# A two-layer hybrid-attention block on one core: silu(c) left in PSUM for the opening, rotary rows doubled in the latent heads, modulation steps regrouped

## The chip, the cores and the metric

The kernel runs on one core of one Trainium2 chip. A time is device microseconds of that core for one execution of the whole program. Engines go by the profile's names: PE is TensorE (PEld its weight loads), DVE VectorE, ACT ScalarE, POOL GpSimd, SP SyncE, which issues every DMA of this kernel.

## What is computed

Two layers over 512 positions of width 1024, batch 1. Each layer has a modulated norm, four groups of attention heads of four heads each, an output product, a second modulated norm and an MLP of 4096 columns with a squared ReLU; a plain norm ends the program. What the change touches is the modulation, the first norm, the latent heads (MLA) and the compressed branch (NSA). The modulation is six parts per layer, each 1024 numbers:

```python
silu(c) @ w_ada[l] + b_ada[l]        # parts 1 and 0: scale and shift of the first norm
h = x * rsqrt(mean(x*x) + 1e-6) * g * (1 + scale) + shift

def mla_mixer(z, q_norm_g, kv_norm_g, w_uq, w_ukv):
    cq, ckv, k_pe = split_last(z, [MLA_Q_RANK, MLA_KV_RANK, MLA_ROPE])     # 192, 128, 32
    q = heads(rmsnorm(cq, q_norm_g) @ w_uq, MLA_HEADS)                     # 4 heads of 64 + 32
    kv = heads(rmsnorm(ckv, kv_norm_g) @ w_ukv, MLA_HEADS)
    q = concatenate([q[..., :64], rope(q[..., 64:], pos)], axis=-1)
    k = concatenate([kv[..., :64], broadcast(rope(k_pe, pos))], axis=-1)
    v = kv[..., 64:]
    return causal_attention_blocks(q, k, v, (64 + 32) ** -0.5)

def compress(t, pos_emb, w1, w2):      # NSA: 31 blocks of 32 positions, stride 16
    blk = overlapping_blocks(t) + pos_emb
    return gelu(blk.reshape(B, n_cmp, 32 * 64) @ w1) @ w2
```

## The kernel before

Activations are kept transposed: 128 features on the partitions, 512 positions along the row, eight such tiles for the width of 1024. Every wide product is done in three: a float32 operand is split into a rounded half (`hi`) and the rest (`lo`), and TensorE adds hi x hi, lo x hi and hi x lo in one PSUM bank (lines 331 to 333 in `mm3`). For weights the split is `W._split`: ScalarE copies the raw tile to `whi` (L89) and GpSimd, or VectorE, subtracts to `wlo` (L91). The raw tiles come through four buffers, one DMA each, all in SyncE's queue; a load waits there until a buffer's last reader is done.

The scheduler of the language sets each engine's order when the program is built, from the order of the code, and each engine then works its list strictly in turn.

The opening (`start`) loads x, sums the squares of its eight tiles (ScalarE squares into PSUM, VectorE adds, `sqacc`), sums over partitions on TensorE (`nsum`), takes the power -0.5 on GpSimd (`rs`, L257) and spreads it over the partitions on TensorE (`rsb`). In parallel it makes the two modulation parts that the first norm needs. One modulation step (`ada_cols`, L188) multiplies a 128x1024 tile of weights with silu(c) in every partition, sums along the row and adds the bias: one column of `mod`. silu(c) is spread over the partitions by eight small products into PSUM (`cbp`, L173), and VectorE copies it to SBUF (`cb`, L177). For tile k of h: two steps, one `gs` (norm weight times 1 + scale, 128x1, L1116), one `ht` = x * gs * rsb (L1122), then on ScalarE `hhi` = ht + shift rounded (L1125), and `hlo` = the rest, on GpSimd for the first five tiles (L1128) and on VectorE for the last three (L1130). Five projections (`pss`, five PSUM banks) are accumulated as the tiles come, 120 products in all. After them comes `proj_N`, whose first product is L503.

The latent heads follow. `cq_evac` turns 32 rows of k_pe: cos on one copy, sin on another, an add, a split into rows 64 to 96 of `cq[1]`. `mla_k` writes one head's key halves `mkh` and `mkl`: 64 rows from the product and 32 rotary rows copied from `cq[1]` by VectorE casts (L755, L756). `mla_q` copies 64 rows, multiplies two sets of 32 rows by cos and sin and adds them (L769 to L772), and splits. Scores are products over 96 rows (L784 to L786). `softmax` is VectorE (bias and minimum, L536), ScalarE (exponential, L541), VectorE (reciprocal), a scaling; `pv` transposes on TensorE, splits on ScalarE and VectorE, and multiplies with v (L590, L591). `kcvc_evac` adds position embeddings to the 31 overlapping blocks on VectorE, eight instructions per layer (L669). Other modulation steps, one 512 KB weight tile each, are placed by hand after heads and projections of layer 0 (`ada_step`; `NOUT` says how many go behind each output product).

## Time and profile before

| | |
|---|---|
| three runs | 1318.11 us median (1315.22 to 1322.64) |
| the profiled execution | 1317.07 us, span 1315.3 us, mean granted clock 0.986 |
| TensorE busy | 1244.1 us, 95% of the span |
| VectorE, ScalarE, GpSimd busy | 725.4, 588.3, 512.9 us |

The span runs from the first to the last instruction of the core; the rest of the execution lies around it. A matmul's busy time is longer than the distance to the next, since they are pipelined. A row of the timeline reads: start, duration, engine, line, operation, output<-inputs, shapes, count, and in brackets the engine's idle time before it with what ended it. A row of a group reads: line, engine, operation, names, shapes, count | busy us, mean ns | idle before. A row of waits reads: total us, times, longest.

### The profile page before, as it was taken

The numbers are of one execution on the slowest core, as the hardware profiler recorded it, in microseconds if no ns is written. First come the engines' busy times: TensorE is split into PE (matmuls) and PEld (weight loads), VectorE is DVE, ScalarE is ACT, GpSimd is POOL, SyncE is SP. The second block draws the span as 40 slices with busy tenths as digits, with TensorE's granted clock in tenths as the row PEclk, the third lists the DMA queues.
The fourth block names the chain that finished last, engine by engine and source line by source line (L and its number), as shares of the span: only waits on it lengthen the run. The fifth ranks groups of instructions, "written<-read, shape, count | busy, mean of one in ns | idle before, by whom it ended". The sixth has DMA issues, their size and how long they took to land. (4 is left out here: it accounts for less than half of the span.)

```text
span 1315.3 us, 17552 instructions
## 1 busy us (share of the span) xinstructions
PE 1244.1 (95%) x6500; PEld 1039.2 (79%) x6500; DVE 725.4 (55%) x1609; ACT 588.3 (45%) x1145; POOL 512.9 (39%) x276
## 2 busy tenths in 40 slices
PE   4997999989999999999998999999999999999997
PEld 3785787769788888888898677877988888888886
DVE  6887968976445455454164887787553312213114
ACT  4355858763433232231234567687343313223220
POOL 5433222333444545445435233232444444444440
PEclk9988999999999999999999999999999999999998
DMA  8633233444346766766323311121422333333211
GB/s 340 212 102 130 78 96 113 161 144 177 96 147 187 242 210 204 244 193 204 130 91 115 114 63 53 61 65 58 136 81 96 96 96 97 96 97 96 96 48 65
DMA packets 49765, 168.68 MB, mean 128 GB/s; under 512 B 5648, under 2 KB 8336, under 8 KB 49680
## 3 DMA queue, kind: packets, MB, share of 16 engines
q1 hardware_dynamic: 49680, 167.57, 38.8%
q8 instruction: 51, 0.84, 0.2%
q14 instruction: 34, 0.28, 0.1%
HBM read 163.35 MB, written 4.19 MB: 127 GB/s over the span
## 5 line engine op out<-in xcount | busy, mean ns | idle before, releaser
L91 POOL TENSOR_TENSOR wlo<-raw,whi 128x1024 fp32r<-128x1024 f32 (+3 forms) x186 | 455.9, 2456 | 570.8 <-ACT whi L89 539.6
L89 ACT ACTIVATE whi<-raw 128x1024 fp32r<-128x1024 f32 (+3 forms) x186 | 193.5, 1045 | 444.4 <-PE px L332 247.0
L331 PE MATMUL pj<-hhi,whi 128*128 128x512 f32 (+1 forms) x783 | 294.0, 377 | 8.5 <-DVE t L1072 5.1
L333 PE MATMUL pj<-hhi,wlo 128*128 128x512 f32 (+1 forms) x783 | 292.8, 375 | 0.0
L332 PE MATMUL pj<-hlo,whi 128*128 128x512 f32 (+1 forms) x783 | 292.5, 374 | 0.0
L331 PE MATMUL px<-a,whi 128*128 128x512 f32 (+1 forms) x560 | 208.6, 372 | 0.0
L333 PE MATMUL px<-a,wlo 128*128 128x512 f32 (+1 forms) x560 | 208.2, 372 | 0.0
L332 PE MATMUL px<-a,whi 128*128 128x512 f32 (+1 forms) x560 | 207.2, 370 | 0.0
L331 PEld LDWEIGHTS pj<-hhi,whi 128*128 128x128 f32 x783 | 148.0, 189 | 33.9 <-DVE t L1072 5.5
L332 PEld LDWEIGHTS pj<-hlo,whi 128*128 128x128 f32 x783 | 148.0, 189 | 25.3 <-DVE hlo L1130 0.3
L333 PEld LDWEIGHTS pj<-hhi,wlo 128*128 128x128 f32 x783 | 147.6, 189 | 25.7
L369 DVE SCALAR_TENSOR_TENSOR x<-px,mod,x 128x512 f32<-128x512 f32 (+1 forms) x92 | 62.1, 680 | 190.2 <-PE px L333 181.1
L1072 DVE SCALAR_TENSOR_TENSOR t<-pj,r 128x512 f32<-128x512 f32 x64 | 44.1, 691 | 159.8 <-ACT r L1071 159.6
L188 DVE CUSTOM_DVE_ANT_0 adaw<-adaw,cb,vecs 128x1024 f32<-128x1024 f32 x78 | 105.7, 1355 | 45.6 <-DMA adaw<-in_wadaD 45.5
L333 PEld LDWEIGHTS px<-a,wlo 128*128 128x128 f32 x560 | 105.1, 188 | 19.2
L332 PEld LDWEIGHTS px<-a,whi 128*128 128x128 f32 x560 | 105.1, 188 | 18.9
L331 PEld LDWEIGHTS px<-a,whi 128*128 128x128 f32 x560 | 105.2, 188 | 17.9
L400 DVE TENSOR_TENSOR a<-t,a 128x512 fp32r<-128x512 f32 x64 | 74.7, 1169 | 41.8 <-ACT a L399 41.8
L541 ACT ACTIVATE e<-e,nm 128x256 f32<-128x256 f32 (+3 forms) x160 | 85.9, 539 | 14.5 <-DVE nm L536 14.4
L519 POOL TENSOR_SCALAR e<-e,rc 128x128 f32<-128x128 f32 x40 | 24.3, 606 | 136.0 <-DVE rc L546 66.2
L400 DVE TENSOR_TENSOR pl<-pt,ph 128x512 fp32r<-128x512 f32 (+1 forms) x112 | 65.3, 597 | 3.5 <-ACT ph L399 2.4
L575 PE MATMUL pt<-ident,e 128*128 128x128 f32 x376 | 61.2, 276 | 3.2 <-DVE pl L400 1.1
(236 smaller groups left out, 1875.9 us busy)
## 6 DMA issues: line engine op xcount, KB each, us to landing
adaw<-in_wadaD SPq DMA_DIRECT2D x78, 512.0 KB, 4.4
raw<-in_wup SPq DMA_DIRECT2D x64, 512.0 KB, 3.5
raw<-in_wdown SPq DMA_DIRECT2D x64, 512.0 KB, 3.5
raw<-in_winT SPq DMA_DIRECT2D x28, 512.0 KB, 3.5
ada<-in_wadaP SPq DMA_DIRECT2D x16, 512.0 KB, 8.5
raw<-in_wout SPq DMA_DIRECT2D x16, 512.0 KB, 3.5
x<-in_xT SPq DMA_DIRECT2D x8, 512.0 KB, 5.5
cw<-in_cw SPq DMA_DIRECT2D x8, 512.0 KB, 4.8
```

The lines of the kernel that those rows point to most:

```text
L89: self.nc.scalar.activation(vh[0:rows], raw[0:rows], AF.Copy)
L91: eng.tensor_tensor(vl[0:rows], raw[0:rows], vh[0:rows].bitcast(F32), op=ALU.subtract)
L188: nc.vector.tensor_tensor_reduce(out=w, in0=w, in1=cb, scale=1.0, scalar=vecs[:, off : off + 1], op0=ALU.mult, op1=ALU.add, accum_out=mod[ ...
L331: nc.tensor.matmul(ps, wh[:, k, :], hh[:, c], start=first, stop=False)
L332: nc.tensor.matmul(ps, wh[:, k, :], hl[:, c], start=False, stop=False)
L333: nc.tensor.matmul(ps, wl[:, k, :], hh[:, c], start=False, stop=last)
L369: last["dve"] = nc.vector.scalar_tensor_tensor(X["x"][:, m, c], ps, mod[l][:, part, m : m + 1], X["x"][:, m, c], op0=ALU.mult, op1=ALU.add)
L400: last["dve"] = nc.vector.tensor_tensor(lo, src, hi.bitcast(F32), op=ALU.subtract)
L519: nc.gpsimd.tensor_scalar_mul(e, e, r)
L541: nc.scalar.activation(e, e, AF.Exp, bias=nm[:, n : n + 1], scale=-1.0, accum_out=den[:, n : n + 1])
L575: nc.tensor.transpose(pt[:, c : c + P], p[n][:, col : col + P], ident)
L1072: nc.vector.scalar_tensor_tensor(t, ps, 0.0, r, op0=ALU.max, op1=ALU.mult)
```

## The change

Opening. silu(c) stays in PSUM (`cbP`, two banks that the score banks take later); the 16 steps of the opening read it there, and ScalarE copies it to SBUF afterwards for all later steps. The squares go to other banks and the weight splits' GpSimd halves stand behind the power. `gs` is made on ScalarE as g * mod + g. `ht` stands behind both steps of its tile. The 120 products are done in another order, with the lo-weight products spread over the tiles.

Latent heads. The 32 rotary key rows are written twice, to rows 64 to 96 and 96 to 128, by SBUF to SBUF DMAs, and each head's copies are DMAs too. The query is not added up: all 128 rows are multiplied by a table (`cs`, ones in the first 64 rows) in PSUM, and the scores run over 128 rows, so the sum is made by the product.

Compressed branch. ScalarE copies the blocks; the position embedding becomes a 32nd column that GpSimd copies in, and the constant `csum` adds it to all blocks.

Modulation steps. The one after the first latent head moves to the first window head, and one more stands behind the output products.

```diff
-NOUT = (1, 1, 1, 1, 0, 0, 0, 0)
+NOUT = (1, 1, 2, 1, 1, 0, 0, 0)
...
-    def ada_cols(w, l, part, m):
+    def ada_cols(w, l, part, m, cv=cb):
...
-        nc.vector.tensor_tensor_reduce(
-            out=w, in0=w, in1=cb, scale=1.0, scalar=vecs[:, off : off + 1],
+        last["ada"] = nc.vector.tensor_tensor_reduce(
+            out=w, in0=cv, in1=w, scale=1.0, scalar=vecs[:, off : off + 1],
...
                         split(hi[64:96], lo[64:96], kr[64:96])
+                        for t in (hi, lo):
+                            nc.sync.dma_start(t[96:128].bitcast(F32), t[64:96].bitcast(F32))
...
-                    nc.gpsimd.memset(cB[kv][:, :, 31:32], 0.0)
+                    po_ = vb + OFF_POS + 16 * kv
+                    nc.gpsimd.tensor_copy(cB[kv][:, :, 31:32], vecs[:, po_ : po_ + 16].unsqueeze(2))
...
-                            nc.vector.tensor_tensor(
+                            nc.scalar.activation(
                                 cB[kv][64 * par : 64 * par + 64, 8 * half : 8 * half + 8, 0:31],
-                                v[:, par, :, half : half + 31],
-                                vecs[r, po_ : po_ + 8].unsqueeze(2).to_broadcast([64, 8, 31]),
-                                op=ALU.add,
+                                v[:, par, :, half : half + 31], AF.Copy,
                             )
...
+                    nc.sync.dma_start(kh[64:128].bitcast(F32), krh[64:128].bitcast(F32))
+                    nc.sync.dma_start(kl[64:128].bitcast(F32), krl[64:128].bitcast(F32))
                     nc.scalar.activation(kh[0:64], ps[r], AF.Copy)
                     nc.vector.tensor_tensor(kl[0:64], ps[r], kh[0:64].bitcast(F32), op=ALU.subtract)
-                    nc.vector.tensor_copy(kh[64:96], krh[64:96].bitcast(F32))
-                    nc.vector.tensor_copy(kl[64:96], krl[64:96].bitcast(F32))
...
-                nc.scalar.activation(f[0:64], ps[0:64], AF.Copy)
-                nc.vector.tensor_tensor(f[64:96], ps[64:96], cs[64:96], op=ALU.mult)
-                nc.vector.tensor_tensor(f2[64:96], ps[96:128], cs[96:128], op=ALU.mult)
-                nc.vector.tensor_tensor(f[64:96], f[64:96], f2[64:96], op=ALU.add)
+                nc.vector.tensor_tensor(ps, ps, cs, op=ALU.mult)
...
-                split(qh[0:96], ql[0:96], f[0:96])
+                split(qh, ql, ps)
...
-            ada_step(1, last["dve"])
             if l:
                 proj_T(hs, [kcvc_evac])
...
+                if h == 0:
+                    ada_step(1, last["dve"])
             flush()
...
+        psC = cps.enter_context(tc.tile_pool(name="psC", bufs=1, space=PSUM))
+        cbP = psC.tile([P, D], F32, name="cbP")
...
+        for k in range(1, KT):
+            sq = mmbank("sq")
+            nc.scalar.activation(sq, X["x"][:, k, :], AF.Square)
+            nc.vector.tensor_tensor(acc, acc, sq, op=ALU.add)
...
-                ws.append(W.get())
-            nc.vector.scalar_tensor_tensor(
-                gs[:, k : k + 1], mod[0][:, 1, k : k + 1], 1.0, vecs[:, OFF_NMIX + k : OFF_NMIX + k + 1],
-                op0=ALU.add, op1=ALU.mult,
+                with tc.issue_after(last["pow"].ins):
+                    ws.append(W.get())
+            g = vecs[:, OFF_NMIX + k : OFF_NMIX + k + 1]
+            nc.scalar.activation(
+                gs[:, k : k + 1], mod[0][:, 1, k : k + 1], AF.Identity, bias=g, scale=g
             )
...
+        nc.scalar.activation(cb, cbP, AF.Copy)
+        cps.close()
+        psS = ctx.enter_context(tc.tile_pool(name="psS", bufs=2, space=PSUM))
...
+        for k in range(KT - 1):
+            for w, j, h in ((0, k, 0), (0, k - 1, 1), (1, k - 2, 0)):
+                if j >= 0:
+                    for g in range(n):
+                        part(g, w, j, h)
```

On GpSimd, at the opening's start, this stood before (`rs` is the power, `wlo` a weight split's lo half):

```order
L91 TENSOR_TENSOR wlo_208<-raw_138,whi_207 128x1024
L91 TENSOR_TENSOR wlo_212<-raw_140,whi_211 128x1024
L257 TENSOR_TENSOR rs<-rsv,mhalf 128x4
L91 TENSOR_TENSOR wlo_231<-raw_205,whi_230 128x1024
L1128 TENSOR_TENSOR hlo<-ht,hhi 128x512
L91 TENSOR_TENSOR wlo_235<-raw_226,whi_234 128x1024
L91 TENSOR_TENSOR wlo_239<-raw_228,whi_238 128x1024
L1128 TENSOR_TENSOR hlo<-ht,hhi 128x512 x4
```

and this stands there now:

```order
L246 TENSOR_TENSOR rs<-rsv,mhalf 128x4
L89 TENSOR_TENSOR wlo_205<-raw_122,whi_204 128x1024
L89 TENSOR_TENSOR wlo_209<-raw_124,whi_208 128x1024
L89 TENSOR_TENSOR wlo_228<-raw_202,whi_227 128x1024
L1130 TENSOR_TENSOR hlo<-ht,hhi 128x512
L89 TENSOR_TENSOR wlo_232<-raw_223,whi_231 128x1024
L89 TENSOR_TENSOR wlo_236<-raw_225,whi_235 128x1024
L1130 TENSOR_TENSOR hlo<-ht,hhi 128x512 x4
```

The power moved ahead of the first two splits; nothing else on GpSimd changed its place here.

On VectorE, in layer 0 from the last key split of NSA to the first latent scores' softmax, before (`VM` the values of the latent heads, `mkl` and `mql` lo halves):

```order
L488 TENSOR_TENSOR VM<-mv,VM 128x4x64 x4
L755 CAST mkh<-cqh_472 32x512
L754 TENSOR_TENSOR mkl<-mk,mkh 64x512
L756 CAST mkl<-cql_473 32x512
L755 CAST mkh<-cqh_472 32x512
L754 TENSOR_TENSOR mkl<-mk,mkh 64x512
L770 TENSOR_TENSOR qf<-mq,cs 32x512
L771 TENSOR_TENSOR qf_742<-mq,cs 32x512
L770 TENSOR_TENSOR qf<-mq,cs 32x512
L772 TENSOR_TENSOR qf<-qf,qf_742 32x512
L771 TENSOR_TENSOR qf_759<-mq,cs 32x512
L400 TENSOR_TENSOR mql<-qf,mqh 96x512
```

and now:

```order
L477 TENSOR_TENSOR VM<-mv,VM 128x4x64 x4
L746 TENSOR_TENSOR mkl<-mk,mkh 64x512
L759 TENSOR_TENSOR mq<-mq,cs 128x512
L746 TENSOR_TENSOR mkl<-mk,mkh 64x512
L389 TENSOR_TENSOR mql<-mq,mqh 128x512
L759 TENSOR_TENSOR mq<-mq,cs 128x512
L525 ISA e_769,nm<-sc,maskL,qsc 128x128
```

The casts are gone, and one product over all rows stands where three instructions stood. On TensorE the 15 products of another projection that stood between the last `mq` product and the first score product `sc` now stand behind the first scores.

On SyncE, the row copies stand among the loads of layer 0 like this (`raw` are weights, `cw` the compression weights, `adaw` modulation weights):

```order
L637 DMA cqh_474<-cqh_474 32x512
L637 DMA cql_475<-cql_475 32x512
L72 DMA raw_667<-in_winT 128x1024
L743 DMA mkh<-cqh_474 64x512
L744 DMA mkl<-cql_475 64x512
L743 DMA mkh<-cqh_474 64x512
L744 DMA mkl<-cql_475 64x512
L205 DMA adaw<-in_wadaD 128x1024
L72 DMA raw_881<-in_winT 128x1024
L798 DMA cw_918<-in_cw 128x192
L743 DMA mkh<-cqh_474 64x512 x2
```

All rows with `mkh`, `mkl`, `cqh` and `cql` are new in this queue; the loads keep their order. The second pair of `mkl` copies follows one load later, with the rest of the loads behind it.

More of the change, by code (lines that the diff above doesn't have):

```diff
@@ L25 @@
 PRELOAD = 2
-KG = 5
 NSPLIT = 3
@@ L118, in layer_stack @@
     psA = ctx.enter_context(tc.tile_pool(name="psA", bufs=3, space=PSUM))
-    psS = ctx.enter_context(tc.tile_pool(name="psS", bufs=2, space=PSUM))
     psT = ctx.enter_context(tc.tile_pool(name="psT", bufs=2, space=PSUM))
     psO = ctx.enter_context(tc.tile_pool(name="psO", bufs=1, space=PSUM))
+    psS = None
     def mmbank(name):
@@ L168, in layer_stack, with ada_start @@
     cb = cons.tile([P, D], F32, name="cb")
-    for half in range(2):
-        ps = psA.tile([P, 512], F32, tag="mm", name="cbp")
-        for j in range(4):
-            k = 4 * half + j
-            nc.tensor.matmul(
-                ps[:, j * P : (j + 1) * P], cact[:, k : k + 1].to_broadcast([P, P]), ident,
-                start=True, stop=True,
-            )
-        nc.vector.tensor_copy(cb[:, 512 * half : 512 * half + 512], ps)
     mod = [cons.tile([P, 6, KT], F32, name=f"mod{l}") for l in range(DEPTH)]
     W = Weights(nc, rawp, hlp, 3, 3)
-    def ada_cols(w, l, part, m):
+    def ada_cols(w, l, part, m, cv=cb):
         off = l * VL + OFF_BADA + 8 * part + m
-        nc.vector.tensor_tensor_reduce(
-            out=w, in0=w, in1=cb, scale=1.0, scalar=vecs[:, off : off + 1],
+        last["ada"] = nc.vector.tensor_tensor_reduce(
+            out=w, in0=cv, in1=w, scale=1.0, scalar=vecs[:, off : off + 1],
             op0=ALU.mult, op1=ALU.add, accum_out=mod[l][:, part, m : m + 1],
         )
-    def ada_start(pool, m):
+    def ada_start(pool, m, cv):
         raw = pool.tile([P, 2, 1024], F32, tag="ada0", name="ada0", bufs=4)
@@ L256, in rstd_cols @@
         r = smp.tile([P, 8], F32, tag="rs", name="rs")
-        nc.gpsimd.tensor_tensor(r[:, 0:n], v[:, 0:n], mhalf[:, 0:n], op=ALU.pow)
+        last["pow"] = nc.gpsimd.tensor_tensor(r[:, 0:n], v[:, 0:n], mhalf[:, 0:n], op=ALU.pow)
         return r
@@ L1093, in start @@
             W._load()
+        cps = ctx.enter_context(ExitStack())
+        psC = cps.enter_context(tc.tile_pool(name="psC", bufs=1, space=PSUM))
+        cbP = psC.tile([P, D], F32, name="cbP")
         for k in range(KT):
-            sums.add(k)
+            nc.tensor.matmul(
+                cbP[:, k * P : (k + 1) * P], cact[:, k : k + 1].to_broadcast([P, P]), ident,
+                start=True, stop=True,
+            )
+        acc = wkp.tile([P, S], F32, tag="sqacc", name="sqacc", bufs=1)
+        nc.scalar.activation(acc, X["x"][:, 0, :], AF.Square)
+        for k in range(1, KT):
+            sq = mmbank("sq")
+            nc.scalar.activation(sq, X["x"][:, k, :], AF.Square)
+            nc.vector.tensor_tensor(acc, acc, sq, op=ALU.add)
         rsb = psO.tile([P, 512], F32, tag="po", name="rsb0")
-        ps = sbank("nsum")
+        ps = psT.tile([P, 512], F32, tag="pt", name="nsum")
         for j in range(NQ):
             nc.tensor.matmul(
-                ps[:, j : j + 1], sums.acc[:, j * P : (j + 1) * P], ones, start=True, stop=True
+                ps[:, j : j + 1], acc[:, j * P : (j + 1) * P], ones, start=True, stop=True
             )
@@ L1121, in start @@
             hi, lo = hs[k]
-            last["dve"] = nc.vector.scalar_tensor_tensor(
-                t, X["x"][:, k, :], gs[:, k : k + 1], rsb, op0=ALU.mult, op1=ALU.mult
-            )
+            with tc.issue_after(last["ada"].ins):
+                last["dve"] = nc.vector.scalar_tensor_tensor(
+                    t, X["x"][:, k, :], gs[:, k : k + 1], rsb, op0=ALU.mult, op1=ALU.mult
+                )
             nc.scalar.activation(hi, t, AF.Identity, bias=mod[0][:, 0, k : k + 1])
@@ L1144, in start, with part @@
             ada_state["i"] += 2
-        for k in range(KG):
-            for g in range(n):
-                nc.tensor.matmul(pss[g], ws[g][0][:, k, :], hs[k][0], start=k == 0, stop=False)
-            for g in range(n):
-                nc.tensor.matmul(pss[g], ws[g][0][:, k, :], hs[k][1], start=False, stop=False)
-            for j in [k] if k >= KD else range(KD) if k == KD - 1 else []:
-                for g in range(n):
-                    nc.tensor.matmul(pss[g], ws[g][1][:, j, :], hs[j][0], start=False, stop=False)
+        def part(g, w, k, h):
+            nc.tensor.matmul(
+                pss[g], ws[g][w][:, k, :], hs[k][h], start=(k + w + h == 0),
+                stop=(k == KT - 1 and w == 1),
+            )
+        for k in range(KT - 1):
[3 more added lines that the diff above has]
+                        part(g, w, j, h)
+        k = KT - 1
         for g in range(n):
-            for k in range(KG, KT):
-                mm3(pss[g], ws[g], hs[k], k, False, k == KT - 1)
+            for w, j, h in (
+                (0, k - 1, 1), (1, k - 2, 0), (1, k - 1, 0), (0, k, 0), (0, k, 1), (1, k, 0)
+            ):
+                part(g, w, j, h)
         return hs, pss
@@ L1218, in _shape_constants @@
     cs = np.zeros((P, S), f)
+    cs[0:64] = 1
     cs[64:80], cs[80:96] = cos, cos
```

26 lines of the change are left out of this document (11 added, 15 removed).

## The prediction, as it was made before the result was known

> **What bounds the kernel now.** I read the page first, then the busy time by stretches, then TensorE's waits, and only then the timeline of the two stretches that the waits point to.
>
> ```profile
> span 1315.3 us, 17552 instructions
> PE 1244.1 (95%) x6500; PEld 1039.2 (79%) x6500; DVE 725.4 (55%) x1609; ACT 588.3 (45%) x1145; POOL 512.9 (39%) x276
> ...
> 30.00:40.00 10.00, 6.64 (x21) 4.72 (x21) 9.93 (x15) 2.89 (x4) 6.22 (x4) 0.83 0.59 200
> ...
> 80.00:128.00 48.00, 40.21 (x232) 31.22 (x231) 38.85 (x90) 27.47 (x64) 12.82 (x10) 0.89 0.36 121
> 700.00:772.00 72.00, 65.15 (x403) 53.00 (x402) 55.05 (x124) 38.92 (x84) 27.75 (x20) 0.98 0.32 107
> 1000.00:1100.00 100.00, 100.00 (x437) 81.93 (x436) 24.16 (x28) 31.01 (x39) 43.20 (x18) 1.00 0.31 96
> ```
>
> The columns of a stretch are its length, then PE, PEld, DVE, ACT and POOL busy, TensorE's granted clock, the DMA engines' share and GB/s. In most of the program (1000 to 1100 us) TensorE is busy without a break, and nothing on another engine counts. The change touches three stretches that are not like that: the opening, where VectorE is full (9.93 of 10 us) and TensorE is not; the latent heads of layer 0 (80 to 128 us: TensorE 40.21 of 48 us, at a clock of 0.89); and those of layer 1 (65.15 of 72 us, 0.98). The most that can be won is what TensorE loses there. TensorE's waits up to 135 us name who is late:
>
> ```profile
> PE nsum L1099 <- DVE sqacc L247: 6.3, 1, 6.3
> PE pj L1149 <- POOL hlo L1128: 3.8, 3, 2.7
> PE rsb L263 <- POOL rs L257: 3.6, 1, 3.6
> PE po L590 <- ACT ph L399: 3.1, 1, 3.1
> PE mq L764 <- DVE q L462: 2.0, 1, 2.0
> ```
>
> The first three are the opening, the last two the latent heads. The opening in order of time:
>
> ```profile
> 9.80 5.46 SPq L74 DMA_DIRECT2D raw<-in_winT  x2
> ...
> 11.43 1.04 ACT L89 ACTIVATE whi<-raw 128x1024 fp32r<-128x1024 f32 x1
> ...
> 12.55 4.67 POOL L91 TENSOR_TENSOR wlo<-raw,whi 128x1024 fp32r<-128x1024 f32 x2 [11.55 <-ACT whi L89]
> 12.99 0.69 DVE L247 TENSOR_TENSOR sqacc<-sqacc,sq 128x512 f32<-128x512 f32 x1 [0.55 <-ACT sq L246]
> ...
> 15.70 0.16 DVE L253 TENSOR_SCALAR rsv<-nsum 128x4 f32<-128x4 f32 x1 [2.03 <-PE nsum L1099]
> ...
> 17.17 1.99 POOL L257 TENSOR_TENSOR rs<-rsv,mhalf 128x4 f32<-128x4 f32 x1
> ...
> 21.34 0.75 DVE L1122 SCALAR_TENSOR_TENSOR ht<-x,gs,rsb 128x512 f32<-128x512 f32 x1 [1.64 <-PE rsb L263]
> ...
> 29.42 2.19 DVE L1116 SCALAR_TENSOR_TENSOR gs<-mod,vecs 128x1 f32<-128x1 f32 x1
> ...
> 31.55 1.29 POOL L1128 TENSOR_TENSOR hlo<-ht,hhi 128x512 fp32r<-128x512 f32 x1
> ...
> 38.99 3.66 PE L1152 MATMUL pj<-hhi,wlo 128*128 128x512 f32 x15
> ...
> 43.12 1.28 DVE L188 CUSTOM_DVE_ANT_0 ada<-ada,cb,vecs 128x1024 f32<-128x1024 f32 x1
> ...
> 55.22 0.75 DVE L1122 SCALAR_TENSOR_TENSOR ht<-x,gs,rsb 128x512 f32<-128x512 f32 x1
> ...
> 61.84 0.28 PE L503 MATMUL pn<-whi,hhi 128*128 128x268 f32 x1
> ```
>
> The eighth tile of h is made at 55.22 and the first projections end at 61.84. VectorE's instructions between 15 and 58 us, in groups:
>
> ```profile
> L188 DVE CUSTOM_DVE_ANT_0 ada<-ada,cb,vecs 128x1024 f32<-128x1024 f32 x16 | 24.8, 1568 | 0.0
> L1116 DVE SCALAR_TENSOR_TENSOR gs<-mod,vecs 128x1 f32<-128x1 f32 x8 | 7.2, 900 | 0.1
> ```
>
> A `gs` works on one column and takes 900 ns, and 2.19 us at 29.42; a modulation step takes 1568 ns here and 1.28 at 43.12. These have two operands in SBUF, and they are long when GpSimd runs a `wlo` or `hlo`. The instructions with one operand in PSUM are not: the `sqacc` add at 12.99 takes 0.69 us in the middle of the `wlo` pair of 12.55 to 17.22. So VectorE loses 24.8 - 16 x 1.28 = 4.3 us on the steps and all 7.2 us on `gs` to GpSimd.
>
> **A: the opening.** (1) The last squares add ends at 12.99 + 0.69 = 13.68. Two copies of silu(c) leave VectorE's queue ahead of it:
>
> ```profile
> L177 DVE COPY cb<-cbp 128x512 f32<-128x512 f32 x2 | 1.4, 682 | 0.0
> ```
>
> and the weight split on ScalarE that stood before the last square (1.04 us at 11.43) goes behind it. The two overlap; I take 1.6 us of the 2.4, so 12.1. (2) The power on GpSimd could start at 15.9 (`rsv` 15.70 + 0.16) and started at 17.17, behind two `wlo`. It now stands first: start 14.3. It took 1.99 us for 4 columns; 2 columns take 0.70 and 8 take longer elsewhere:
>
> ```profile
> L257 POOL TENSOR_TENSOR rs<-rsv,mhalf x11: 695/697/1994, 17.2 to 1306.8; 128x2 f32<-128x2 f32 x8, 128x8 f32<-128x8 f32 x2, 128x4 f32<-128x4 f32 x1
> ```
>
> I take 1.6, inside these bounds: end 15.9 instead of 19.16, and the first `ht` at 18.1 instead of 21.34. (3) GpSimd then does, in its new order, three `wlo`, the first `hlo`, two `wlo`, the second `hlo`: 5 x 2.33 + 2 x 1.3 = 14.3, so the second `hlo` is ready at 30.2 instead of 32.84. This is what TensorE waits for. (4) VectorE per tile: two steps of 1.28 and one `ht` of 0.75, 3.3 us where it is 4.8 now ((55.22 - 21.34) / 7). Seven tiles and two `hlo` of 0.75 put the eighth `ht` at 18.1 + 23.1 + 1.5 = 42.7. The loads cost some of that: SyncE stood 5.46 us at 9.80 for the buffer that the first `wlo` frees, and that `wlo` now ends at 18.2 instead of 14.9; I add 1.6 us, half of that, for a dry DMA queue: 44.3. ScalarE has two splits of winA and the copy of cb ahead of the eighth `hhi`, each at most the 1.04 us of a 1024-column split; they start before that `ht`, so the `hhi` is ready by 47. (5) TensorE has 100 of its 120 products left at 30.2: 100 x 0.244 (3.66 / 15) = 24.4, and about 0.9 more while its clock is low, half of what the 0.83 of 30 to 40 us costs now. End: 55.5 instead of 61.84, **-6.3 us**. The eighth tile is needed 25 products before the end, at 49.4; it is there 2 us earlier. Bounds: -3 if the second `hlo` comes no earlier and only the stalls behind it go (61.84 - 32.84 = 29.0 for 104 products, of which 25.4 are work); -9 if the power takes 0.70 and the clock is full.
>
> The steps now read silu(c) from PSUM, which no step here does. Nearest rows: a subtraction from PSUM in `pl` and one with both in SBUF in `olo`:
>
> ```profile
> 104.81 1.29 DVE L400 TENSOR_TENSOR pl<-pt,ph 128x512 fp32r<-128x512 f32 x2 [0.70 <-ACT ph L399]
> L400 DVE TENSOR_TENSOR olo<-o,ohi 128x512 fp32r<-128x512 f32 x16 | 11.0, 686 | 1.6 <-ACT ohi L399 1.6
> ```
>
> 0.65 against 0.69 us: no price. [...]
>
> **B: the latent heads of layer 0.** The groups that go (both layers), and the place where one of them costs TensorE most:
>
> ```profile
> L669 DVE TENSOR_TENSOR cB<-pj,vecs 64x248 f32<-64x248 f32 x16 | 6.6, 412 | 0.2
> L756 DVE CAST mkl<-cql 32x512 fp32r<-32x512 f32 x8 | 6.0, 753 | 0.2
> L755 DVE CAST mkh<-cqh 32x512 fp32r<-32x512 f32 x8 | 5.9, 737 | 0.1
> L771 DVE TENSOR_TENSOR qf<-mq,cs 32x512 f32<-32x512 f32 x8 | 5.6, 696 | 0.1
> L772 DVE TENSOR_TENSOR qf<-qf,qf 32x512 f32<-32x512 f32 x8 | 5.4, 680 | 0.2
> ...
> 99.04 2.38 POOL L91 TENSOR_TENSOR wlo<-raw,whi 128x1024 fp32r<-128x1024 f32 x1 [3.69 <-ACT whi L89]
> 99.27 2.43 DVE L756 CAST mkl<-cql 32x512 fp32r<-32x512 f32 x1
> ...
> 102.58 0.72 ACT L541 ACTIVATE e<-e,nm 128x512 f32<-128x512 f32 x1 [2.15 <-DVE nm L536]
> ...
> 104.83 0.80 PE L590 MATMUL po<-ph,VM 128*128 128x512 f32 x1 [3.11 <-ACT ph L399]
> ```
>
> 6.6 + 6.0 + 5.9 + 5.6 + 5.4 = 29.5 us of VectorE work go, about half in each layer; the one product with `cs` on 128 rows replaces one on 32 rows of the same 512 columns. One more modulation step (1.28 us) moves out of the latent stretch. In 80 to 128 us VectorE is the fullest of the helpers (38.85 of 48), so this counts. The clearest piece is the cast at 99.27: held by the `wlo` of 99.04 it takes 2.43 us, the last softmax step comes late, ScalarE idles 2.15 us, and TensorE 3.11. With the cast made a DMA I take 2.4 of these 3.11. Of the 2.0 us for `q` I take half (the casts and the longer q chain ahead of it go, the contended step stays). The low clock (0.89 over 48 us is 5.3 us of lost clock, about half of it recoverable when the waits shrink) I take at 2.1. **-5.5 us**; bounds 0 (the waits are chains and not VectorE's load) and -12.9 (all 7.8 us of idle and 5.1 of clock). [...]
>
> **C: the latent heads of layer 1**: the same edits without modulation steps, and TensorE has 6.9 us idle in 72. I take a third of it, **-2.5 us**; bounds 0 and -6.9.
>
> **D: what is added.** Eight copies of 64x248 per layer on ScalarE, by the 412 ns that they took on VectorE 3.3 us, lie in its idle time (27.47 busy of 48); if that cover went, 3.3 us. The step moved to the first window head, 1.28 us: VectorE is full there, I take half. TensorE's fill work (15 products) no longer stands between the q products and the first scores, so TensorE meets the q chain bare: 0.4. **+1.0 us**, bounds 0 and +4. The row copies of rotary keys are ten DMAs a layer (64 to 128 KB) in SyncE's queue among the weight loads. The nearest transfer lands in 2.9 us:
>
> ```profile
> raw<-in_wukv SPq DMA_DIRECT2D x2, 256.0 KB, 2.9
> ```
>
> The first two pairs are issued once `cqh` and `cql` have their rotary rows, ahead of the products of VA and VM, so these hide them and I cost them at nothing.
>
> **Sum.** -6.3 - 5.5 - 2.5 + 1.0 = -13.3. The profiled execution took 1317.07 (span 1315.3 and 1.8 around it), the three runs have a median of 1318.11, 1.0 above it. 1317.07 - 13.3 = **1303.8 us**.
>
> **Rivals.** *Only the opening pays*: the latent stretches are chains of softmax steps, ScalarE has its eight copies in the chain, and B and C come to nothing: 1317.07 - 6.3 + 1.0 = 1311.8. For it: ScalarE and TensorE wait for each other there too. Against: the 2.43 us cast is plainly in the path. *The opening hangs on the loads*: the later first `wlo` holds the queue, the stream runs dry for longer than 1.6 us, and the opening gives 3 us: 1307.1. Against it: DMA was busy only 0.59 in 30 to 40 us. *More*: the power takes 0.70 us and the clock stays full, A -9, B -9: 1317.07 - 19.5 = 1297.6. *Slower*: the second pair of `mkl` copies needs buffers that earlier heads read, so SyncE stands until their scores are done, with weights, cw1 and biases queued behind, and each head's scores wait for a copy's landing: 8 heads x 2.9 = 23 us while B and C pay nothing: 1317.07 - 6.3 + 23 = 1334. It decides only once the copies are issued after q is ready, and costs more than the opening gains from the third head on.
>
> **Chances.** Forecast 0.60, only the opening 0.14, loads 0.10, more 0.10, slower 0.04, else 0.02. Half a per cent, 6.6 us, is about what a measurement of this kernel can tell from no change: faster means below 1311.5. Forecast and loads nearly all fall there, the first rival by a little less than half: faster 0.83, same 0.12, slower 0.05. Range: the bounds of the unknown costs, cut to 8 in 10, 1296 to 1312.
>
> **What would show it.** `gs` gone from VectorE, the steps at 1.25 to 1.3 us with GpSimd at work beside them; the second `hlo` ready near 30 us and the last product of the opening near 55.5 us; no VectorE instruction over 2 us in the latent stretches but the two steps on cb in SBUF; TensorE's wait for `ph` under 1 us; granted clock in the latent stretch over 0.89. Wrong if steps reading PSUM still stretch beside GpSimd, if TensorE waits for `mkh` or `mkl`, or if the opening's gain is lost again before 130 us.

## The result, and the profile after

The changed kernel took 1309.59 us (median of 6 runs, 1306.48 to 1311.24), the kernel before, beside it, 1321.56 us: ratio 0.9916, 95% interval 0.9892 to 0.994. Run again beside later experiments it took 1308.25 us, ratio 0.9907 (0.9885 to 0.9929). Its profiled execution took 1309.58 us (span 1307.8), 7.5 us less than that of before, which was one of the faster runs of its kernel (1315.1 to 1326.7 over all).

The page of the changed kernel, its busy times:

```profile
span 1307.8 us, 17559 instructions
...
PE 1242.6 (95%) x6500; PEld 1039.7 (80%) x6500; DVE 685.9 (52%) x1551; ACT 594.5 (45%) x1162; POOL 508.9 (39%) x276
```

The opening of the changed kernel, in order of time:

```profile
11.39 1.48 DVE L1096 TENSOR_TENSOR sqacc<-sqacc,sq 128x512 f32<-128x512 f32 x2
...
15.20 1.02 POOL L246 TENSOR_TENSOR rs<-rsv,mhalf 128x4 f32<-128x4 f32 x1 [14.20 <-DVE rsv L242]
16.18 7.01 POOL L89 TENSOR_TENSOR wlo<-raw,whi 128x1024 fp32r<-128x1024 f32 x3
...
18.44 0.75 DVE L1124 SCALAR_TENSOR_TENSOR ht<-x,gs,rsb 128x512 f32<-128x512 f32 x1 [0.99 <-ACT whi L87]
...
25.26 1.28 DVE L177 CUSTOM_DVE_ANT_0 ada<-cbP,ada,vecs 128x1024 f32<-128x1024 f32 x1 [3.00 <-DMA ada<-in_wadaP]
...
29.05 2.58 POOL L1130 TENSOR_TENSOR hlo<-ht,hhi 128x512 fp32r<-128x512 f32 x2
...
29.30 1.99 PE L1151 MATMUL pj<-hhi,whi 128*128 128x512 f32 x5 [1.86 <-ACT hhi L1127]
...
31.09 2.33 PE L1151 MATMUL pj<-hlo,whi 128*128 128x512 f32 x5
...
44.41 0.74 DVE L1124 SCALAR_TENSOR_TENSOR ht<-x,gs,rsb 128x512 f32<-128x512 f32 x1
...
55.34 0.28 PE L492 MATMUL pn<-whi,hhi 128*128 128x268 f32 x1
```

The second `hlo` is ready at 29.05 + 1.30 = 30.35, the eighth `ht` starts at 44.41, and the first VA product starts at 55.34 instead of 61.84. TensorE's waits up to 135 us (us in total, times, longest; `csc` are the scores of the compressed branch, `mq` and `mv` the products that make the latent heads' q and values):

```profile
PE nsum L1100 <- DVE sqacc L1096: 5.5, 1, 5.5
PE pj L1151 <- ACT hhi L1127: 3.8, 3, 1.9
...
PE csc L866 <- ACT kc L388: 1.6, 1, 1.6
PE mq L754 <- DVE q L451: 1.5, 1, 1.5
PE mv L725 <- DVE VM L477: 1.5, 1, 1.5
```

and the same three stretches as in the prediction:

```profile
30.00:40.00 10.00, 10.00 (x38) 7.95 (x37) 10.00 (x17) 4.84 (x10) 4.24 (x4) 0.83 1.03 409
80.00:128.00 48.00, 44.13 (x259) 34.27 (x258) 31.84 (x92) 29.67 (x70) 12.76 (x10) 0.92 0.37 116
700.00:772.00 72.00, 64.90 (x383) 53.13 (x382) 40.09 (x109) 39.27 (x92) 22.89 (x18) 0.93 0.37 110
```

The wait for `ph` (3.1 us) is gone from the list; VectorE fell from 38.85 to 31.84 us in the stretch of layer 0 and from 55.05 to 40.09 us in that of layer 1. But in layer 1 TensorE does no more work in its 72 us than before (64.90, was 65.15), at a lower clock (0.93, was 0.98). The same program lies 6 to 8 us earlier now, so a fixed stretch does not hold quite the same work in both kernels.

So the same marks were read from TensorE's timeline in every profile: the start of the first VA product (the opening's end), and the time from it to the first `mk`, from there to the first `pct` transpose (the latent heads), from there to the last of layer 0's output products (selected branch, window heads, output product), and `mk` to `pct` in layer 1. In us:

| kernel | opening | VA to mk | latent, layer 0 | pct to output | latent, layer 1 |
|---|---|---|---|---|---|
| before | 61.84 | 21.98 | 58.43 | 172.32 | 58.40 |
| changed | 55.34 | 21.95 | 53.56 | 176.14 | 59.70 |
| changed, again (c_after) | 53.97 | 22.06 | 51.75 | 176.33 | 58.45 |
| e1_opening | 53.90 | 21.88 | 57.30 | 174.48 | 60.28 |
| e2_latent | 61.81 | 22.00 | 50.99 | 174.86 | 58.80 |
| e3_no_regroup | 53.36 | 22.08 | 51.16 | 172.24 | 58.41 |
| e4_kc_dve | 53.99 | 21.59 | 53.53 | 179.46 | 55.45 |
| x5_noreg_kc | 55.01 | 23.57 | 50.80 | 174.16 | 58.10 |
| x6_warm | 54.01 | 23.34 | 53.96 | 176.66 | 57.27 |
| x7_noreg_mv | 54.14 | 19.47 | 48.79 | 172.97 | 58.69 |
| x8_cmpkv_first | 54.89 | 19.51 | 46.77 | 172.72 | 57.90 |
| o1_sbuf_steps | 61.70 | 21.72 | 50.78 | 177.87 | 57.20 |
| o2_power_behind | 54.56 | 23.68 | 52.07 | 176.74 | 58.81 |
| o3_old_order | 54.69 | 22.24 | 51.14 | 177.35 | 58.50 |

Kernels alike in a stage differ there by 1 to 3 us from one profile to another; the experiment on the clock bears on it. In the two profiles of the changed kernel the opening gave 6.5 and 7.9 us, layer 0's latent heads 4.9 and 6.7, layer 1's nothing, and 3.8 to 4.0 us went back between `pct` and the output product. Between `mk` and `pct` of layer 0 the granted clock is 0.91 before, 0.90 in the changed kernel and 0.95 in c_after; in layer 1 it is 0.97, 0.92 and 0.95.

### The profile page after: what moved, and what is told of

Read it like the earlier page. It is cut to its first block, busy times and chain, and to the rows that moved or that the text cites. A ratio compares the mean times of both kernels' runs of the same rounds, so it can differ in the third digit from the quotient of the medians.

```text
span 1307.8 us, 17559 instructions
## 1 busy us (share of the span) xinstructions
PE 1242.6 (95%) x6500; PEld 1039.7 (80%) x6500; DVE 685.9 (52%) x1551; ACT 594.5 (45%) x1162; POOL 508.9 (39%) x276
## 5 line engine op out<-in xcount | busy, mean ns | idle before, releaser
L320 PE MATMUL pj<-hhi,whi 128*128 128x512 f32 (+1 forms) x768 | 288.0, 376 | 7.1 <-DVE t L1060 5.1
L322 PE MATMUL pj<-hhi,wlo 128*128 128x512 f32 (+1 forms) x768 | 286.4, 374 | 0.0
L321 PE MATMUL pj<-hlo,whi 128*128 128x512 f32 (+1 forms) x768 | 285.4, 372 | 0.0
L320 PEld LDWEIGHTS pj<-hhi,whi 128*128 128x128 f32 x768 | 144.9, 189 | 30.2 <-DVE t L1060 5.5
L322 PEld LDWEIGHTS pj<-hhi,wlo 128*128 128x128 f32 x768 | 144.8, 189 | 24.9
L321 PEld LDWEIGHTS pj<-hlo,whi 128*128 128x128 f32 x768 | 145.1, 189 | 24.5
L177 DVE CUSTOM_DVE_ANT_0 adaw<-cb,adaw,vecs 128x1024 f32<-128x1024 f32 x78 | 104.6, 1340 | 46.6 <-DMA adaw<-in_wadaD 46.4
```

Of the source, the lines that this page charges most:

```text
L177: last["ada"] = nc.vector.tensor_tensor_reduce(out=w, in0=cv, in1=w, scale=1.0, scalar=vecs[:, off : off + 1], op0=ALU.mult, op1=ALU.add, ...
L320: nc.tensor.matmul(ps, wh[:, k, :], hh[:, c], start=first, stop=False)
L321: nc.tensor.matmul(ps, wh[:, k, :], hl[:, c], start=False, stop=False)
L322: nc.tensor.matmul(ps, wl[:, k, :], hh[:, c], start=False, stop=last)
```

## The experiments

**Each part alone.** Before with the opening alone:

```diff
+        cbP = psC.tile([P, D], F32, name="cbP")
...
+            ada_start(pool, k, cbP)
...
+                gs[:, k : k + 1], mod[0][:, 1, k : k + 1], AF.Identity, bias=g, scale=g
```

> The kernel before with the opening of the change alone (silu(c) in PSUM, scale columns on ScalarE, power ahead of the weight splits, new order of products); latent heads and modulation steps as before. Theory (the terms add): first product behind the opening at 55.3 instead of 61.84 us, that -6.5 kept to the end, ratio to the kernel before 0.995. Rival (what the opening wins is given back later, because the stages behind it are chains or wait for loads whatever arrives early): the same -6.5 at the first product of VA, but under -3 at the end, ratio 0.998 or more.

1311.28 us, ratio 0.9927 (0.9897 to 0.9956): the theory's 0.995 lies within the interval, the rival's 0.998 outside it. In its profile the opening is 7.9 us shorter and the end comes 4.2 us earlier. The rest is missing behind the opening, where this profile lost 21.8 us at half clock and that of before 16.4 (how this is counted is said under the clock, below). Its latent heads keep the old wait for `ph`:

```profile
96.83 0.79 PE L579 MATMUL po<-ph,VM 128*128 128x512 f32 x1 [3.11 <-ACT ph L388]
```

Before with the latent heads alone:

```diff
+                    nc.sync.dma_start(kh[64:128].bitcast(F32), krh[64:128].bitcast(F32))
...
+                nc.vector.tensor_tensor(ps, ps, cs, op=ALU.mult)
...
+                                v[:, par, :, half : half + 31], AF.Copy,
```

> The kernel before with the latent heads of the change alone (rotary rows copied by DMA, q made in PSUM, the eight position adds as copies on ScalarE); opening and modulation steps as before. Theory (terms add): nothing up to the first mk product, 5 to 6 us won between it and the compressed scores (csc) of layer 0, nothing in layer 1, ratio 0.995 to 0.997. Rival (the 6 us belong to the modulation step that left the latent heads): under 3 us won up to csc. Rival (layer 1's loss of clock comes of the opening's shift): 2 us won in layer 1 here.

1309.85 us, ratio 0.9917 (0.9891 to 0.9944). The latent heads of layer 0 are 7.4 us shorter, more than expected (1.7 of it is less time at half clock), with the modulation step still among them, and layer 1's are not (58.80). So the gain is that of the edits to the heads and not of the step that left, and layer 1's nothing does not come of the opening's shift. The two parts alone are worth 0.73% and 0.83%, together without the rest 1.29%, all three parts 0.84 to 0.93%. The third part, the regrouping, costs time.

**The regrouping undone.**

```diff
-NOUT = (1, 1, 2, 1, 1, 0, 0, 0)
+NOUT = (1, 1, 1, 1, 0, 0, 0, 0)
             mla_head(0)
+            ada_step(1, last["dve"])
...
-                if h == 0:
-                    ada_step(1, last["dve"])
```

> The changed kernel with the modulation steps where they were (one back behind the first latent head, none in the first window head, two at the end of the window heads, four instead of six in the output product). Theory (the moved steps are what gives 5 us back between csc and the output product of layer 0): 1 to 2 us later at csc, but 3 to 5 us less is lost behind it, so 2 to 3 us faster than the changed kernel, ratio to before 0.989 or less. Rival (the regrouping pays or is neutral; the loss behind csc is the clock or the chain of softmax steps): as fast as the changed kernel or up to 2 us slower, ratio 0.992 to 0.994, with the same loss behind csc.

1304.51 us, ratio 0.9871 (0.9846 to 0.9896). The stage from `pct` to the output product takes 172.2 to 174.9 us (mean 173.4) in the seven profiles without the regrouping and 176.1 to 179.5 (mean 177.2) in the seven with it, without overlap: 3.8 us. The clock is not the cause: with what half clock lost taken off (counted as under the clock, below), the two groups are 170.6 to 173.2 and 174.3 to 176.3 us. The latent heads, out of which a step was moved, are no slower with it (51.16 here, 51.75 in c_after). Two losses can be seen. TensorE's waits from 205 to 310 us in c_after (the changed kernel):

```profile
...
PE px L320 <- ACT ohi L388: 1.7, 2, 1.3
...
PE rsb L252 <- POOL rs L246: 1.4, 1, 1.4
```

VectorE's and GpSimd's timeline there:

```profile
272.25 0.69 DVE L389 TENSOR_TENSOR olo<-o,ohi 128x512 fp32r<-128x512 f32 x1 [0.69 <-ACT ohi L388]
...
295.77 1.28 DVE L177 CUSTOM_DVE_ANT_0 adaw<-cb,adaw,vecs 128x1024 f32<-128x1024 f32 x1
...
295.94 1.70 POOL L246 TENSOR_TENSOR rs<-rsv,mhalf 128x2 f32<-128x2 f32 x1 [5.78 <-DVE rsv L242]
```

The same waits and the same instructions in e3_no_regroup:

```profile
...
PE rsb L252 <- POOL rs L246: 0.9, 2, 0.5
...
PE px L320 <- ACT ohi L388: 0.2, 1, 0.2
```

```profile
267.92 0.69 DVE L389 TENSOR_TENSOR olo<-o,ohi 128x512 fp32r<-128x512 f32 x1 [0.70 <-ACT ohi L388]
...
291.63 0.73 POOL L246 TENSOR_TENSOR rs<-rsv,mhalf 128x2 f32<-128x2 f32 x1 [5.78 <-DVE rsv L242]
```

One step that went into the output product stands beside the norm's power on GpSimd: the power takes 1.70 instead of 0.73 us, and TensorE waits 1.4 instead of 0.5. (There were two more steps in the output product, `NOUT` 6 instead of 4, where two had followed the window heads; the section on the change counted one.) And the last `olo` comes 47.5 us after the first output product (224.71) instead of 44.8 (223.15): 2.8 us, and TensorE waits 1.7 us for `ohi` where it waits 0.2 in e3. Together that is 3.7 us of the 4.1 by which the stage differs between these two profiles (176.33 and 172.24). That the last window head ends later is shown; which of the moved steps makes the instructions of its tail come out in that order was not tried.

**The position adds back on VectorE**, in the changed kernel and without the regrouping.

```diff
-                            nc.scalar.activation(
+                            nc.vector.tensor_tensor(
...
-                                v[:, par, :, half : half + 31], AF.Copy,
+                                v[:, par, :, half : half + 31],
+                                vecs[r, po_ : po_ + 8].unsqueeze(2).to_broadcast([64, 8, 31]),
+                                op=ALU.add,
```

> The changed kernel with the eight adds of cB back on VectorE, with their position rows (the rows of the copies on ScalarE and the extra column go). Theory (the copies on ScalarE cost nothing, 3.3 us of VectorE's work per layer count): 1 to 3 us slower than the changed kernel over both layers, ratio to before 0.992 to 0.994. Rival (ScalarE's copies stand in the softmax chain of layer 1 and ate what the forecast put at -2.5 there): layer 1 1 to 3 us faster, ratio under 0.991.

1303.10 us, ratio 0.9871 (0.9836 to 0.9906). To tell whether this adds to the last:

> The changed kernel with both put back: modulation steps where they were, and the position adds of cB on VectorE. Theory (two losses of their own, in different stages): 8 to 11 us faster than the changed kernel, ratio to before 0.983 to 0.985. Rival (one and the same spread, or a loss that shows only where the clock's windows happen to fall): no faster than the changed kernel without the regrouping, 0.987 or more.

1305.46 us, 0.9886 (0.9859 to 0.9912), no faster than e3; and the changed kernel itself beside it:

> The changed kernel once more, on the chip of its neighbours here, so that they can be compared with it. If the 1304.5 us without the regrouping and the 1303.1 us with the position adds on VectorE are gains of those edits, it stays at 0.9916 of the kernel before (1309 to 1311 us); if they were the spread of six runs each, it comes out at 0.987 to 0.989 here.

1308.25 us. The medians do not part the two edits. Without the regrouping the ratio is 0.9871 with the adds on ScalarE and 0.9886 with them on VectorE; with the regrouping it is 0.9907 to 0.9916 and 0.9871, so that with the adds on VectorE the regrouping seems to cost nothing. The traces part them. From `pct` to the output product the regrouping costs in both pairs (179.46 us in e4 against 174.16 in x5). And the copies on ScalarE cost time in layer 1, as the rival of e4 had it. In the changed kernel all eight run there in one block, and four exponentials and then `ph` (L388) come behind it:

```profile
727.04 3.05 ACT L661 ACTIVATE cB<-pj 64x248 f32<-64x248 f32 x8
...
732.83 1.09 ACT L388 ACTIVATE ph<-pt 128x512 fp32r<-128x512 f32 x2
```

In e4 `ph` comes right behind its transpose:

```profile
729.09 1.09 ACT L388 ACTIVATE ph<-pt 128x512 fp32r<-128x512 f32 x2 [0.25 <-PE pt L564]
```

TensorE waits 1.4 us for `ph` there in each of the ten profiles with the copies, and in none of the four without them (before, e1, e4, x5). Layer 1's 55.45 us in e4 were not seen again in x5 (58.10), because x5 lost 4.4 us at half clock there and e4 1.0. The changed kernel's first profile lost 4.6 us there, about as much as x5, and took 59.70: 1.6 us more.

**The clock.** In the changed kernel single windows of 3.41 us run at half clock. TensorE's activity in two windows and their successors in c_after (after the length: PE, PEld, DVE, ACT and POOL busy, clock, DMA):

```profile
71.50:74.91 3.41, 1.48 (x8) 1.07 (x8) 2.21 (x4) 2.50 (x7) 3.41 (x3) 0.99 0.52 149
74.91:78.33 3.42, 3.11 (x9) 2.63 (x10) 1.50 (x5) 0.97 (x2) 1.76 (x1) 0.51 0.86 249
112.40:115.80 3.40, 1.82 (x11) 1.27 (x9) 2.59 (x4) 2.71 (x5) 3.40 (x2) 1.00 0.04 12
115.80:119.20 3.40, 3.40 (x10) 2.68 (x9) 1.58 (x8) 1.00 (x4) 1.79 (x2) 0.50 0.83 230
```

Each of these half-clock windows follows one in which TensorE is idle about half of the time, here by the 1.5 us wait of `mv` and the 1.6 us wait of `csc`. To fill such waits without taking them away:

```diff
+                if j == 3:
+                    warm = psT.tile([P, 512], F32, tag="pt", name="warm")
+                    for _ in range(6):
+                        nc.tensor.matmul(warm, hs[0][0][:, 0:P], hs[0][0], start=True, stop=True)
                 ps = mmbank("mv")
...
+            for _ in range(6):
+                nc.tensor.matmul(cst, hs[0][0][:, 0:P], hs[0][0], start=True, stop=True)
```

> The changed kernel with six products of no use (512 columns, 0.23 us each) put into TensorE's queue at four places where it waits 1.4 to 1.6 us: ahead of the last mv product, which waits for a PSUM bank, and ahead of csc, which waits for kc, in both layers. Nothing is removed from any wait. Theory (a window of 3.4 us in which TensorE idles about half is followed by one at half clock, 1.7 us of lost work each): the half-clock windows behind these four places are gone from the trace, and it is 3 to 6 us faster than the changed kernel. Rival (the clock does not hang on idling of this length): as many half-clock windows, and 0 to 2 us slower, for the useless products.

1306.11 us, ratio 0.9887 (0.986 to 0.9913), 2.1 us faster than c_after, with overlapping intervals. The stretches of x6_warm around `mv` and `csc` of layer 0:

```profile
71.60:75.01 3.41, 2.84 (x21) 2.54 (x20) 0.69 (x2) 3.29 (x8) 2.62 (x2) 1.00 0.14 14
75.01:78.43 3.42, 2.85 (x16) 2.22 (x15) 2.88 (x6) 1.20 (x4) 3.35 (x2) 1.00 0.66 234
...
115.80:119.20 3.40, 3.40 (x19) 2.83 (x17) 1.29 (x2) 2.99 (x4) 1.90 (x1) 1.00 0.01 2
```

Useless products at those places keep the clock at 1.00 there, and layer 1's half-clock windows behind `mv` and `csc` (709.7 and 757.5 in c_after) are gone too. But others appeared at 59 and 100 us, where c_after had none: behind the opening the profile of x6_warm lost 17.6 us at half clock, that of c_after 14.3. The gain is under the expected 3 to 6 us and not clear of the noise.

What half clock loses is counted here as half of the time that the trace shows at half clock; where TensorE also waits, that is an upper bound. The windows lie on a grid (in the changed kernel's first profile half-clock windows begin at 29.92, 60.64 and 77.71 us, 9 and 5 lengths of 3.413 us apart), and the grid lies differently from run to run (in c_after the one behind `mv` begins at 74.91, 2.80 us and so no whole length from 77.71). Which wait falls into one window with another differs with it. This makes most of the 1 to 3 us between profiles of like kernels: from layer 0's last output product to layer 1's first `mk`, work that twelve of the fourteen kernels share (x7 and x8 below change `mv`), it takes 405.0 to 410.0 us, and with the 0 to 5.9 us lost at half clock taken off 404.1 to 405.2.

One half-clock window of c_after follows one that the profile shows as busy without a break:

```profile
685.85:689.25 3.40, 3.40 (x26) 3.14 (x26) 1.21 (x4) 0.20 (x1) 0.92 (x1) 1.00 0.48 158
689.30:692.70 3.40, 3.40 (x10) 2.63 (x9) 2.63 (x5) 0.62 (x1) 1.96 (x2) 0.50 0.15 30
```

Of its 26 products 19 are `mlas`, sums over partitions with a single column each. Thirteen of the fourteen profiles have such a case, sixteen in all, and in each the window before holds 19 to 24 of these products. So these narrow products seem to count little for the clock, by these sixteen cases; no run here tests that by itself.

**The waits themselves taken away**, without the regrouping: `mv` in more PSUM banks,

```diff
-                ps = mmbank("mv")
+                ps = mmbank("mv") if j < 2 else psT.tile([P, 512], F32, tag="pt", name="mv")
```

> The changed kernel without the regrouping, and with the third and fourth mv product of each layer in the two PSUM banks of the pt ring instead of behind the three of the mm ring. Theory: the 1.4 to 1.5 us wait of mv for VM goes in both layers, and with it a half-clock window of 1.7 us where one followed: 3 to 6 us faster than without the regrouping alone (1304.5 us, 0.9871), 0.983 to 0.985 of before. Rival (the first mk product waits for the same evacuations, so the wait only moves): within 1 us of it.

1297.64 us, ratio 0.983 (0.9807 to 0.9852): the theory, with 6.9 us a little more than expected. Part of the wait moved, as the rival had it: `mq` now waits 0.9 us (layer 0) and 1.0 us (layer 1) for `VM`. From VA to `mk` it takes 19.47 us instead of 22, and no half-clock window is left between 56 and 131 us (nor in x8, next; the other kernels have 2 to 5 there). Then also the compressed keys before the fourth head's q, and `mv` in three rings:

```diff
+                ps = (
+                    mmbank("mv") if j == 0 else sbank("mv") if j == 1
+                    else psT.tile([P, 512], F32, tag="pt", name="mv")
+                )
...
-            mla_q(3)
             cps = mmbank("cmpkv")
...
             split(vc[:, :, 0, :], vc[:, :, 1, :], vcf)
+            mla_q(3)
```

> The changed kernel without the regrouping, with the four mv products in four banks of three rings (mm, sc, pt, pt), and with the compressed keys' products and their split ahead of the fourth latent head's q products. Theory: beside what the two mv banks gave (1297.6 us, 0.983), the 1.6 us wait of csc for kc goes in both layers, with a half-clock window behind it where the idling was enough, and the 1.0 us wait behind mv: 3 to 6 us faster, 0.979 to 0.981 of before. Rival (kc waits for something else, or the wait moves to the first scores of the fourth head): within 1.5 us of 1297.6.

1292.79 us, ratio 0.9777 (0.9754 to 0.98), faster than both kernels; by the ratios 1.3% under the changed kernel (0.9777 / 0.9907) and 1.0% under it without the regrouping (0.9777 / 0.9871). TensorE's waits from 683 to 775 us in c_after:

```profile
PE pj L320 <- ACT ckvg L645: 2.0, 1, 2.0
PE cmph L805 <- DMA cw<-in_cw: 1.9, 1, 1.9
PE csc L866 <- ACT kc L388: 1.6, 1, 1.6
PE po L579 <- ACT ph L388: 1.4, 1, 1.4
PE mv L725 <- DVE VM L477: 1.4, 1, 1.4
```

and in x8_cmpkv_first:

```profile
PE cmph L809 <- DMA cw<-in_cw: 1.7, 1, 1.7
PE po L579 <- ACT ph L388: 1.4, 1, 1.4
PE sc L774 <- ACT mqh L388: 1.2, 1, 1.2
PE csc L870 <- DVE kc L389: 0.4, 1, 0.4
```

(The wait for `ckvg` stands ahead of the stage, and in x8 before this window.) The wait for `VM` is gone and that for `kc` is down to 0.4, but the fourth head's scores now wait 1.0 to 1.2 us for their q, as the rival had it: part of the gain moved.

**The opening's parts.** The steps with silu(c) in SBUF, copied by ScalarE before x lands:

```diff
+        nc.scalar.activation(cb, cbP, AF.Copy)
         acc = wkp.tile([P, S], F32, tag="sqacc", name="sqacc", bufs=1)
...
-            ada_start(pool, k, cbP)
+            ada_start(pool, k, cb)
```

> The changed kernel with silu(c) copied to SBUF by ScalarE at once (in its idle time before x lands), and the modulation steps of the opening reading that copy: only the place of one operand differs. Theory (two operands in SBUF make a step wait for GpSimd's splits): steps beside wlo and hlo take 1.9 to 3.4 us again, the mean of the sixteen is 1.5 us or more instead of 1.28, the eighth tile of h comes 3 to 5 us later than 44.4, and the opening ends 0 to 2.5 us later. Rival (the place of the operand does not matter, the steps were long for another reason): mean 1.28 us, opening and total as in the changed kernel.

1314.48 us, ratio 0.9949 (0.9928 to 0.997). The steps as a group in it:

```profile
L177 DVE CUSTOM_DVE_ANT_0 ada<-cb,ada,vecs 128x1024 f32<-128x1024 f32 x16 | 30.0, 1899 | 0.0
```

GpSimd's timeline, and the first VA product on TensorE's:

```profile
15.13 1.92 POOL L246 TENSOR_TENSOR rs<-rsv,mhalf 128x4 f32<-128x4 f32 x1 [14.13 <-DVE rsv L242]
17.02 8.19 POOL L89 TENSOR_TENSOR wlo<-raw,whi 128x1024 fp32r<-128x1024 f32 x3
...
34.03 4.53 POOL L1131 TENSOR_TENSOR hlo<-ht,hhi 128x512 fp32r<-128x512 f32 x2
...
61.70 0.28 PE L492 MATMUL pn<-whi,hhi 128*128 128x268 f32 x1
```

The same group of the changed kernel:

```profile
L177 DVE CUSTOM_DVE_ANT_0 ada<-cbP,ada,vecs 128x1024 f32<-128x1024 f32 x16 | 20.1, 1278 | 3.0 <-DMA ada<-in_wadaP 3.0
```

The place of one operand is worth the whole gain of the opening: 61.70 us where before took 61.84, with everything else of the change in place. Whether that move would give it without the rest was not run. The loss is larger than expected because GpSimd pays too: its power takes 1.92 instead of 1.02 us, three `wlo` 8.19 instead of 7.01, an `hlo` 2.27 instead of 1.30, and the second `hlo` is ready at 34.03 + 2.27 = 36.3 instead of 30.35. Next the rule that holds the weight splits back until the power is issued:

```diff
-                with tc.issue_after(last["pow"].ins):
-                    ws.append(W.get())
+                ws.append(W.get())
```

> The changed kernel without the rule that holds the weight splits back until the power of the norm is issued, so that GpSimd may split weights ahead of it. Theory (the power and the two hlo behind it set when TensorE gets its second hlo, and that sets the end of the opening): the power ends 2 to 4 us later, the first tile of h too, and the opening ends 1 to 3 us later. Rival (GpSimd's whole queue up to the second hlo sets it, whatever stands first): the second hlo is ready at the same 30 us, and the opening ends within 0.5 us of the changed kernel.

1307.31 us, 0.9899 (0.9878 to 0.992). The power still stands first on GpSimd (it starts at 14.96), since ScalarE's squares now precede its weight splits in the program anyway: the edit moved nothing on these two engines, so it tells only that the rule is not needed. And the product order:

```diff
-        for k in range(KT - 1):
-            for w, j, h in ((0, k, 0), (0, k - 1, 1), (1, k - 2, 0)):
...
+        for k in range(KG):
+            for g in range(n):
+                nc.tensor.matmul(pss[g], ws[g][0][:, k, :], hs[k][0], start=k == 0, stop=False)
```

> The changed kernel with the opening's products in the order of the kernel before (for each of five tiles hhi, hlo, then the weights' low parts in a block, and the last three tiles bank by bank). Theory (20 products stand ahead of the second hlo in both orders, so the order is worth nothing): the opening ends within 0.7 us of the changed kernel. Rival (the new order, with hlo one tile and wlo two tiles later, is what lets TensorE work while VectorE and GpSimd are late): 2 to 4 us later.

1310.58 us, 0.9909 (0.9886 to 0.9933), opening 54.69 us, as the theory had it: the order is worth nothing.

## Why the prediction was right or wrong

**The total.** 1303.8 was predicted and 1309.6 measured: the direction and most of the size were right, and it is 5.8 us too low. Of the forecast's ratio (13.3 of 1317.1, 1.0%) the runs show 0.84 to 0.93%; the sum stood on a profiled execution 4 us under the later medians of its kernel.

**A, the opening (-6.3): right in size**, at -6.5 (-7.9 in c_after). (1) The last add ended at 12.87, not 12.1, since ScalarE waited for x. (2) The power took 1.02 and not 1.6 us, which made up for it: first `ht` 18.44 (18.1 forecast). (3) The second `hlo` at 30.35 (30.2), but it is no longer what TensorE waits for: its last wait of the opening is for the third `hhi` (1.86 us, until 29.30), and it takes the second `hlo` at 31.09 without one. The two come within about 1 us of each other, so that the sum held in spite of this is partly luck. (4) The eighth `ht` at 44.41 (44.3), with 3.00 us for the dry load queue instead of 1.6. (5) The end at 55.34 (55.5). The cause is as argued, but wider: with the steps reading PSUM, GpSimd's instructions are shorter as well as VectorE's (changed kernel against o1_sbuf_steps: 1278 against 1899 ns a step, 1.30 against 2.27 us an `hlo`). 5 x 2.33 + 2 x 1.3 held because nothing stretched these any more (three `wlo` in 7.01 us, two in 4.73, two `hlo` in 2.58), which step (3) did not say. A PSUM source showed no price, as the prediction took it: the sixteen steps take 1.27 to 1.28 us with silu(c) in PSUM, and in the kernel before those from 46.35 to 52.6 us, with both operands in SBUF and GpSimd idle, 1.27 to 1.28.

**B, layer 0's latent heads (-5.5): right in kind.** 7.4 us by themselves (58.43 to 50.99), 4.9 to 6.7 in the changed kernel. The `ph` wait went entirely (2.4 of 3.1 had been taken), the q wait from 2.0 to 1.5 (half had been taken), and the wait of `csc` for `kc`, which had no price, from 2.1 to 1.6. The clock's 2.1 us did not come in the changed kernel's first profile: between `mk` and `pct` it lost 5.1 us at half clock, as before did, and the 0.92 against 0.89 of the fixed stretch comes of the stage having moved. c_after lost 2.8. No instruction of VectorE exceeds 1.5 us there now.

**C, layer 1 (-2.5): wrong.** The step that failed is "I take a third" of TensorE's idle time, without naming a wait that VectorE ends. (A third of 6.9 is 2.3; and the stretch was not the stage: in before the latent heads of layer 1 lie from 721.45 to 779.85 us, and TensorE is idle for 4.7 us there.) The waits of before from 690 to 790 us would have shown that hardly any of it was VectorE's:

```profile
PE csc L880 <- ACT kc L399: 2.1, 1, 2.1
...
PE cmph L819 <- DMA cw<-in_cw: 1.8, 1, 1.8
...
PE po L590 <- ACT ph L399: 0.2, 1, 0.2
```

15 us of VectorE work went. The `cw` load stayed (1.9), `kc` fell to 1.6, and `ph` rose to 1.4 because ScalarE's copies now stand ahead of it; that sign of the prediction (`ph` under 1 us) was met in layer 0 and missed here. The clock did the rest: at half clock the stage lost 1.7 us before, 4.6 and 2.9 in the two profiles of the changed kernel. Profiles that lost about as much as each other show what the edits are worth: the changed heads with the copies 0.6 to 1.2 us (59.70 against 60.28 in e1, 57.20 in o1 against 58.40 in before), without the copies 2.2 (58.10 in x5 against 60.28 in e1). With one profile each, this is an estimate. Taking the `mv` wait away shortened this layer ahead of the stage, by 2.4 to 2.8 us from VA to `mk` (13.9 us instead of 16.3 to 16.7).

**D, what is added (+1.0): too small, in two terms.** The regrouping costs 3.8 us and not 0.6. It was priced by the length of one step; the two that went into the output product were given no price at all. And ScalarE's copies do not lie in its idle time: that was read in layer 0's stretch (27.47 of 48 us), but in layer 1 they stand in the softmax chain, with the 1.4 us wait for `ph` behind them. The row copies by DMA cost nothing that can be told: no TensorE wait names `mkh` or `mkl`.

**The rivals.** "Only the opening pays" (1311.8) lies near the time, but for the wrong reason: the latent heads paid 5 to 7 us and the regrouping gave 4 of it back. The sum of A, B and D as measured is -6.5 - 5.8 + 3.8 = -8.5 (B as the mean of both profiles), and the profiles show -7.5 and -10.3. The medians differ by 12.0 us, 3.5 more than these terms; only one execution of before was profiled, so where the rest lies is not known, and that the ratio came so near the forecast, with C giving nothing and D costing 2.8 us more, is partly luck. "Loads" was seen (3.00 us dry) without costing the end; "more" and "slower" were not seen.
